# Place of the turned work and of operand sums behind the weight pieces, with one more buffer, in a two-layer fp32 decoder

## The chip, the cores and the metric

The kernel runs on one core of one Trainium2 chip. Five engines work side by side: TensorE (PE in the profile, with PEld for its weight loads), VectorE (DVE), ScalarE (ACT), GpSimd (POOL) and SyncE (SP). Each takes its own instructions strictly in order. The metric is the device time of one execution, in microseconds (us), median over runs.

## The reference

A decoder of two layers on 256 tokens of width 2048, all in float32. Layer one mixes tokens by gated linear attention (GLA, 4 heads), layer two by causal softmax attention (16 heads); each is followed by a gated feed-forward block with a causal convolution of width 3. Cut to what the change touches:

```python
def gla_mixer(x, ...):
    q, k, v, g = split(rms_norm(x) @ w_in)
    ...                                  # decays, masked scores, values
    o = rms_norm(o, o_norm_w) * silu(g)
    return o @ w_out

def conv_ffn(x, norm_w, w_up, conv_w, conv_b, w_down):
    h = rms_norm(x, norm_w) @ w_up       # 2048 -> 2 * 5632
    acc = conv_b + sum(conv_w[j] * h shifted by 2 - j tokens for j in 0..2)
    a, u = split(acc)
    return (silu(a) * u) @ w_down        # 5632 -> 2048
```

## The kernel before

Nearly all time is matrix products of 256 tokens with weights that come from HBM once, 1 MB at a time (SP issues them, L95, into three buffers `wraw`). Each megabyte holds two **pieces** of 128x1024. A piece is split into two parts of reduced precision: ACT casts it to `whi` (L132), DVE subtracts to get `wlo` (L133), and PE multiplies whi with both parts of the activations and wlo with one. One plain piece is one **step** of 12 matmuls of 512 columns (L281 and L284). `prefetch` traces the casts two pieces ahead of the step, in the down projections three to five.

The down projections (`w_go` after GLA, `w_dn` after each feed-forward block, `w_mo` after attention; matmuls at L692) save products: a megabyte marked `+` in `ORDERS` is multiplied in seven products where others take eight. It needs sums of weight blocks (`t13`, `t24`, made by DVE in `_sums`, L105 to L107, and cast and subtracted as further pieces) and sums of activation blocks (`comb`, made by `combine`, L568 to L571, and split at L294 and L295). For the feed-forward blocks the combs of `EARLY` are made as the activations come out; the others in `combine_parts` (L578 first), at places 2, 4, 6, ... of the down projection's list.

Products come out with tokens on partitions; what follows needs features there. So each result of a step group is scaled to `tok` (ACT; L600 for the gates, L623 for the up projection), transposed in blocks by DVE into `z` (L372, L624), stored to DRAM and loaded back **turned** by POOL's DMA queue (L375 and L381, L628 and L634). Then a job works on the turned tile: `keys`, `queries`, `gated` (ACT L589 into `g`, then split into `go`) and `convolve` (ACT L642, DVE L644 to L649, split into `hid`). `after(n, job)` traces a job n steps later; jobs on turned tiles have n = 6 and more. In GLA `gla_scores` (matmuls `sT`, L526) and `gla_values` (`o`, L543) come 8 and 10 steps behind the queries, the second head of a pair two steps later.

A scheduler then orders the traced instructions on each engine by its own estimate of when operands are there. So the order on an engine may differ from the order of the code, within the dependencies and within the edges that `issue_after` adds: it holds what is traced inside it behind a given instruction on that instruction's engine.

Tiles `slot` are 4 KB per partition from a pool `big` of 34.

## Time and profile before

| what | us |
|---|---|
| median of 3 runs (2234.88 to 2238.73) | 2235.11 |
| the profiled execution | 2234.8 |
| its span, first to last instruction | 2233.0 |
| TensorE busy | 2192.9 |
| VectorE busy | 1585.1 |
| ScalarE busy | 1270.8 |
| mean granted TensorE clock | 0.992 |

The profiled execution lies 0.3 us under the median and has 1.8 us outside its span. The page of the profile lists busy time, the chain of work that ended last and the costliest groups; the trace behind it tells for each instruction how long its engine sat idle ahead of it and what ended that, in square brackets. Such an idle time ahead of a matmul is time of the whole kernel, since PE is the engine that is nearly always busy. PE has few of them, 36 us in all; they stand in the GLA block and at the start of each down projection.

### The profile page before, as it was taken

Reading aid. Unit: us, or ns where it says so; the run is one execution under the profiler, and the core shown is the slowest. Engines: PE = TensorE matmul, PEld = TensorE weight load, DVE = VectorE, ACT = ScalarE, POOL = GpSimd, SP = SyncE. Lnnn points to the kernel's source line nnn. Section 1 sums busy time; section 2 is a strip of 40 time slices with the busy share of each in tenths; the row PEclk is TensorE's granted clock in tenths of the full one; section 3 lists DMA queues with packets and bytes.
Section 4 is the critical chain, followed back from the end, with each engine's and each line's share of the span. In section 5 each row is a group of like instructions: output and inputs, shape, how many; then the busy total and the mean of one; then the engine's idle time right before and its main releaser. Section 6 shows DMA issues by size and latency. Waiting matters only on the chain.

```text
span 2233.0 us, 26994 instructions
## 1 busy us (share of the span) xinstructions
PE 2192.9 (98%) x9805; PEld 1810.5 (81%) x9805; DVE 1585.1 (71%) x2162; ACT 1270.8 (57%) x1812; POOL 263.0 (12%) x368
## 2 busy tenths in 40 slices
PE   9999979999999999999999999999999999999999
PEld 7887857888888888788878888888888888887887
DVE  6655568577767767978856666776676767779886
ACT  6555545565655656555556666555565565655453
POOL 1011111111111111000021000011111111110000
PEclk9999999999999999999999999999999999999999
DMA  8576657777777787566685444486777777774655
GB/s 315 172 224 188 205 173 247 214 242 240 244 243 242 234 249 235 192 220 215 225 284 207 172 169 170 171 253 209 250 238 238 245 242 244 235 241 186 219 215 169
DMA packets 87238, 495.40 MB, mean 222 GB/s; under 512 B 12433, under 2 KB 12961, under 8 KB 37058
## 3 DMA queue, kind: packets, MB, share of 16 engines
q1 hardware_dynamic: 60578, 417.53, 53.9%
q0 software_dynamic: 25952, 75.59, 13.3%
q8 instruction: 76, 1.25, 0.2%
q10 hardware_dynamic: 576, 0.58, 0.1%
q14 instruction: 56, 0.46, 0.1%
HBM read 455.88 MB, written 37.77 MB: 221 GB/s over the span
## 4 chain that ended last, share of the span: by engine, by line
PE 82%; issue 12%; DMA 4%; DVE 1%; POOL 1%; ACT 0%; SPq 0%; DVEq 0%; POOLq 0%; ACTq 0%
PE acc L281 41%; PE acc L284 21%; PE acc L692 11%; PE p L692 7%; DMA c<-rows 1%; DMA wraw<-w_go 1%; DMA turned<-z 1%; DVE wlo L133 1%; POOL upT L634 0%; DMA turned<-queries 0%; PE sT L526 0%; PE o L543 0%; DMA wraw<-w_v 0%; DMA turned<-gates 0%; PE tr L849 0%
## 5 line engine op out<-in xcount | busy, mean ns | idle before, releaser
L133 DVE TENSOR_TENSOR wlo<-wraw,whi 128x1024 fp32r<-128x1024 f32 (+1 forms) x786 | 929.0, 1191 | 458.9 <-ACT whi L132 440.2
L132 ACT CAST whi<-wraw 128x1024 fp32r<-128x1024 f32 (+1 forms) x786 | 799.6, 1027 | 688.5 <-PE acc L281 435.3
L281 PE MATMUL acc<-whi,xw 128*128 128x512 f32 x3840 | 953.7, 390 | 3.6 <-ACT xw L244 1.9
L281 PEld LDWEIGHTS acc<-whi,xw 128*128 128x128 f32 x3840 | 720.8, 188 | 154.7 <-ACT xw L244 3.0
L284 PE MATMUL acc<-wlo,xw 128*128 128x512 f32 x1920 | 514.9, 389 | 0.0
L284 PEld LDWEIGHTS acc<-wlo,xw 128*128 128x128 f32 x1920 | 360.2, 188 | 74.7
L692 PE MATMUL acc<-whi,hid 128*128 128x512 f32 x572 | 185.2, 393 | 2.5 <-DVE c L733 2.5
L692 PE MATMUL p<-whi,hid 128*128 128x512 f32 x506 | 167.5, 393 | 0.0
L281 PE MATMUL acc<-whi,xkv 128*128 128x512 f32 x512 | 133.9, 394 | 0.0
L634 POOL DMA_DIRECT2D upT<-turned x176 | 114.0, 654 | 147.1 <-DMA turned<-z 64.5
L692 PE MATMUL acc<-whi,comb 128*128 128x512 f32 x328 | 109.2, 397 | 20.8 <-ACT whi L132 16.6
L692 PEld LDWEIGHTS acc<-whi,hid 128*128 128x128 f32 x572 | 108.2, 190 | 26.0 <-DVE c L733 3.4
L132 ACT CAST whi<-t 128x1024 fp32r<-128x1024 f32 x82 | 85.3, 1051 | 76.6 <-PE p L692 41.5
L628 POOL DMA_DIRECT2D turned<-z x44 | 34.1, 774 | 679.1 <-DVE z L624 633.0
L133 DVE TENSOR_TENSOR wlo<-t,whi 128x1024 fp32r<-128x1024 f32 x82 | 99.4, 1219 | 19.8 <-PE p L692 9.9
L692 PEld LDWEIGHTS p<-whi,hid 128*128 128x128 f32 x506 | 96.2, 190 | 20.3
L281 PEld LDWEIGHTS acc<-whi,xkv 128*128 128x128 f32 x512 | 94.1, 188 | 18.3
L642 ACT ACTIVATE au<-upT,cs 128x256 f32<-128x256 f32 x176 | 96.0, 595 | 15.8 <-DMA upT<-turned 15.7
L692 PE MATMUL acc<-wlo,hid 128*128 128x512 f32 x286 | 94.8, 390 | 0.0
L692 PEld LDWEIGHTS acc<-whi,comb 128*128 128x128 f32 x328 | 62.5, 191 | 35.9 <-ACT whi L132 18.4
L692 PE MATMUL p<-wlo,hid 128*128 128x512 f32 x253 | 83.8, 390 | 0.0
L724 POOL DMA_DIRECT2D c<-rows x24 | 21.3, 1100 | 520.1 <-DVE c L719 508.2
(241 smaller groups left out, 1931.2 us busy)
## 6 DMA issues: line engine op xcount, KB each, us to landing
wraw<-w_up SPq DMA_DIRECT2D x176, 1024.0 KB, 5.3
wraw<-w_dn SPq DMA_DIRECT2D x88, 1024.0 KB, 5.2
turned<-z POOLq DMA_DIRECT2D x44, 512.0 KB, 3.5
upT<-turned POOLq DMA_DIRECT2D x176, 128.0 KB, 4.9
wraw<-w_g SPq DMA_DIRECT2D x16, 1024.0 KB, 5.1
wraw<-w_go SPq DMA_DIRECT2D x16, 1024.0 KB, 6.1
wraw<-w_mq SPq DMA_DIRECT2D x16, 1024.0 KB, 6.1
wraw<-w_kk SPq DMA_DIRECT2D x16, 1024.0 KB, 4.9
```

The costliest lines, as they stand in the source:

```text
L132: nc.scalar.copy(hi[:, a:b], src[:, a:b])
L133: nc.vector.tensor_sub(lo[:, a:b], src[:, a:b], hi[:, a:b].bitcast(F32))
L281: T.matmul(ps[:, t, :], xs(kt)[:, x0 + 128 * t:x0 + 128 * t + 128], hi[:, c:c + 512], start=kt == 0 and x0 == 0, stop=False)
L284: T.matmul(ps[:, t, :], xs(kt)[:, 128 * t:128 * t + 128], lo[:, c:c + 512], start=False, stop=kt == KT - 1)
L628: nc.gpsimd.dma_start(turned[J].rearrange("(a i) r q c -> (i r) a (q c)", a=4), z.rearrange("p (a q) t c -> p a (q t c)", a=4))
L634: nc.gpsimd.dma_start(f[32 * q:32 * q + 32].rearrange("p a (i c) -> p (a i) c", i=4), turned[J][:, :, q, :].rearrange("a r c -> r a c"))
L642: A.activation(au[:, i, :], t[:, i, :], AF.Identity, bias=col(cb + n), scale=col(cw + 2 * 2 * FT + n))
L692: T.matmul(p[n], x[xi], w[wi][:, 512 * f:512 * f + 512], start=n not in begun, stop=left[n] == 0)
L724: nc.gpsimd.dma_start(r[n], res(n // 2, 2 * b + n % 2), accum_op=OP.add)
```

## The change

Four edits. `behind` puts jobs on turned tiles under edges to the latest traced cast (ACT) and subtraction (DVE), and those jobs are traced one step later (7 for 6). GLA's scores and values come off that list and are placed by themselves: 11 and 14 steps behind the queries for the first head, 13 and 16 for the second (8, 10, 10 and 12 before). The combs of the down projections are traced two places ahead of the megabyte that uses them, instead of at places 2, 4, 6, ...; number 7 joins `EARLY`. `big` has 35 slots.

```diff
-EARLY = (1, 3, 5)
+EARLY = (1, 3, 5, 7)
...
+        self.latest = []
...
+    def behind(self):
+
+        stack = ExitStack()
+        for ins in self.latest:
+            stack.enter_context(self.tc.issue_after(ins))
+        return stack
...
                 with self.tc.issue_after(self.first) if n + a else nullcontext():
-                    nc.scalar.copy(hi[:, a:b], src[:, a:b])
-                nc.vector.tensor_sub(lo[:, a:b], src[:, a:b], hi[:, a:b].bitcast(F32))
+                    one = nc.scalar.copy(hi[:, a:b], src[:, a:b])
+                two = nc.vector.tensor_sub(lo[:, a:b], src[:, a:b], hi[:, a:b].bitcast(F32))
+            self.latest = [one.ins, two.ins]
...
-    big = ctx.enter_context(tc.tile_pool(name="big", bufs=34))
+    big = ctx.enter_context(tc.tile_pool(name="big", bufs=35))
...
+            def run(job):
+                with ws.behind():
+                    job(got["f"])
+
             for lag, job in jobs:
-                after(lag, lambda job=job: job(got["f"]))
+                after(lag, lambda job=job: run(job))
...
-        through(g, z, [(6 + i, lambda f, hd=2 * g + i, i=i: keys(hd, f[:, 2 * i:2 * i + 2])) for i in range(2)])
+        through(g, z, [(7 + i, lambda f, hd=2 * g + i, i=i: keys(hd, f[:, 2 * i:2 * i + 2])) for i in range(2)])
...
-            jobs += [(6 + i, lambda f, hd=hd, i=i: queries(hd, f[:, 2 * i:2 * i + 2])),
-                     (8 + 2 * i, lambda f, hd=hd: gla_scores(hd)),
-                     (10 + 2 * i, lambda f, hd=hd: gla_values(hd))]
+            jobs += [(7 + i, lambda f, hd=hd, i=i: queries(hd, f[:, 2 * i:2 * i + 2]))]
+            after(11 + 2 * i, lambda hd=hd: gla_scores(hd))
+            after(14 + 2 * i, lambda hd=hd: gla_values(hd))
...
-        through(hd, z, [(6 + i, lambda f, c=2 * hd + i: gated(c, f)) for i in range(2)])
+        through(hd, z, [(7 + i, lambda f, c=2 * hd + i: gated(c, f)) for i in range(2)])
...
             au = temp("au")
+            with ws.behind():
+                for i in range(2):
+                    n = i * FT + j
+                    A.activation(au[:, i, :], t[:, i, :], AF.Identity, bias=col(cb + n),
+                                 scale=col(cw + 2 * 2 * FT + n))
             for i in range(2):
                 n = i * FT + j
-                A.activation(au[:, i, :], t[:, i, :], AF.Identity, bias=col(cb + n),
-                             scale=col(cw + 2 * 2 * FT + n))
...
-                after(6 + 2 * i, lambda J=J, i=i: convolve(2 * J + i, f[J][:, 2 * i:2 * i + 2, :]))
+                after(7 + 2 * i, lambda J=J, i=i: convolve(2 * J + i, f[J][:, 2 * i:2 * i + 2, :]))
...
-            for i, k in enumerate(new):
-                todo.setdefault(i if name == "mo" else 2 + 2 * i, []).append(
-                    lambda k=k: combine_parts(k, xs, combos))
+            for k in new:
+                at = next(i for i, (k_, _) in enumerate(order) if k_ == k)
+                todo.setdefault(max(at - 2, 0), []).append(lambda k=k: combine_parts(k, xs, combos))
```

The line numbers move down by 8 at L132, by 9 at L294, by 13 at L589 and L600, by 14 at L642 and by 16 at L718.

**The end of GLA on ACT.** This is ACT's queue where the last gate group ends and the output projection `w_go` begins. `g` is turned work (megabytes 4 and 5 of the gated result), `tok` empties the last gate group out of PSUM, `wraw_2271` is the second megabyte of w_go, `wraw_2305` the third, `t13_2307` and `t24_2308` sums of the second (in the rows of the change too). Before:

```order
L132 CAST whi_2373<-t13_2307 128x1024
L132 CAST whi_2423<-wraw_2305 128x1024
L589 ACTIVATE g_2338<-turned_2246,cs_85 128x256 x2
L589 ACTIVATE g_2362<-turned_2246,cs_85 128x256 x2
L600 ACTIVATE tok_2390<-acc_2214,col_n_524 128x512
L600 ACTIVATE tok_2394<-acc_2214,col_n_524 128x512
L294 CAST go_2341<-g_2338 128x2x256
L132 CAST whi_2344<-wraw_2271 128x1024
```

After, the same place:

```order
L140 CAST whi_2338<-wraw_2271 128x1024
L602 ACTIVATE g_2356<-turned_2246,cs_85 128x256 x2
L140 CAST whi_2322<-wraw_2271 128x512
L303 CAST go_2359<-g_2356 128x2x256
L140 CAST whi_2367<-t13_2307 128x1024
L613 ACTIVATE tok_2384<-acc_2200,col_n_524 128x512
L613 ACTIVATE tok_2388<-acc_2200,col_n_524 128x512
L140 CAST whi_2423<-wraw_2305 128x1024
```

Two of the four `g` moved from ahead of tok to behind it; the two that stay ahead stand two weight pieces earlier than before, behind the wide piece of the second megabyte.

**The first half of w_go on ACT, some ten pieces on.** `t24_2369` (before) and `t24_2363` (after) are the same sums, of the fourth megabyte; `wraw_2348` and `wraw_2342` the fifth megabyte, `wraw_2448` the sixth, `wraw_2468` the seventh. Before:

```order
L132 CAST whi_2464<-wraw_2320 128x1024
L132 CAST whi_2540<-wraw_2448 128x1024
L132 CAST whi_2562<-wraw_2468 128x1024
L589 ACTIVATE g_2487<-turned_2439,cs_85 128x256 x2
L589 ACTIVATE g_2509<-turned_2439,cs_85 128x256 x2
L294 CAST go_2490<-g_2487 128x2x256
L132 CAST whi_2493<-t24_2369 128x1024
L294 CAST go_2512<-g_2509 128x2x256
L132 CAST whi_2531<-wraw_2348 128x1024
```

After:

```order
L140 CAST whi_2464<-wraw_2320 128x1024
L140 CAST whi_2487<-t24_2363 128x1024
L140 CAST whi_2540<-wraw_2448 128x1024
L140 CAST whi_2562<-wraw_2468 128x1024
L602 ACTIVATE g_2503<-turned_2439,cs_85 128x256 x2
L602 ACTIVATE g_2525<-turned_2439,cs_85 128x256 x2
L734 COPY c0_2572<-acc_2450 128x512
L303 CAST go_2506<-g_2503 128x2x256
L303 CAST go_2528<-g_2525 128x2x256
L140 CAST whi_2531<-wraw_2342 128x1024
```

The cast of t24 moved ahead of the casts of the sixth and seventh megabyte; the second piece of the fifth megabyte (`whi_2531`) still stands behind them and behind the turned work.

**The start of a feed-forward down projection on DVE.** These rows end with the second sum of `t24` of the second `+` megabyte (number 3). `whole` and `comb` are the combs of activations, `au` and `hid` the last convolutions. Before:

```order
L568 TENSOR_TENSOR comb_7310<-whole_7308 128x128
L570 TENSOR_TENSOR comb_7310<-whole_7308 128x128
L578 TENSOR_TENSOR whole_7396<-hid_6023 128x512
L106 TENSOR_TENSOR t24_7149<-t13_7148,wraw_7043 128x512
L133 TENSOR_TENSOR wlo_7205<-t13_7148,whi_7204 128x1024
L569 TENSOR_TENSOR comb_7310<-comb_7310,whole_7308 128x128
L133 TENSOR_TENSOR wlo_7187<-wraw_7043,whi_7186 128x1024
L105 TENSOR_TENSOR t13_7237<-wraw_7167 128x1024
L568 TENSOR_TENSOR comb_7398<-whole_7396 128x128
L570 TENSOR_TENSOR comb_7398<-whole_7396 128x128
L295 TENSOR_TENSOR hid_7082<-au_7129,hid_7082 128x256
L107 TENSOR_TENSOR t24_7149<-wraw_7043,t24_7149 128x512
```

After:

```order
L107 TENSOR_TENSOR t24_7137<-t13_7136,wraw_7041 128x512
L584 TENSOR_TENSOR comb_7366<-whole_7364,comb_7366 128x128
L141 TENSOR_TENSOR wlo_7165<-wraw_7041,whi_7164 128x512
L662 SCALAR_TENSOR_TENSOR au_7125<-upT_6993,cs_85,au_7125 128x254
L582 TENSOR_TENSOR comb_7454<-comb_7454,whole_7452 128x128
L141 TENSOR_TENSOR wlo_7175<-wraw_7041,whi_7174 128x1024
L662 SCALAR_TENSOR_TENSOR au_7125<-upT_6993,cs_85,au_7125 128x254
L141 TENSOR_TENSOR wlo_7193<-t13_7136,whi_7192 128x1024
L108 TENSOR_TENSOR t24_7137<-wraw_7041,t24_7137 128x512
```

The third megabyte's first sum (`t13_7237`, 128x1024) moved behind this place, and so did part of the combs. Counted from the subtraction of the half piece of the first `+` megabyte to the row that ends each piece, the new order has 4 `whole` down to 3, 13 additions of 128x128 down to 7, one split of a comb down to none, two sums of 128x1024 down to one, two more small steps of the convolution down to one each, and seven subtractions of a full piece in both. In the up projections the place of each instruction against the weight pieces is the same as before, but for the comb of number 7.

## The prediction

> **What bounds the kernel now.** I read the engines' busy time first, then whom PE waits for, then the five stretches in which its waits lie.
>
> ```profile
> PE 2192.9 (98%) x9805; PEld 1810.5 (81%) x9805; DVE 1585.1 (71%) x2162; ACT 1270.8 (57%) x1812; POOL 263.0 (12%) x368
> PE acc L692 <- ACT whi L132: 16.6, 3, 10.9
> PE acc L692 <- ACT tok L600: 4.1, 1, 4.1
> PE acc L692 <- DVE wlo L133: 3.9, 8, 1.0
> PE sT L526 <- DVE qq L496: 1.9, 1, 1.9
> PE sT L526 <- DVE qq L498: 0.8, 1, 0.8
> ```
>
> PE is the bound, and 27.3 us of its waits stand in these five rows (total, times, longest). The change adds and removes no matmul, so all it can win is waits and what hangs on them. The next view has, for a stretch, the busy time and count of each engine, the granted clock, the DMA share and GB/s: first a quiet stretch of an up projection, then the scores of GLA, the end of GLA with the start of w_go, and the starts of the two feed-forward down projections.
>
> ```profile
> 420.00:520.00 100.00, 100.00 (x443) 82.81 (x442) 69.26 (x98) 56.77 (x79) 14.26 (x21) 1.00 0.74 235
> 184.40:205.50 21.10, 18.36 (x78) 15.25 (x77) 9.88 (x15) 9.28 (x17) 1.05 (x2) 0.84 0.57 176
> 275.60:341.00 65.40, 49.22 (x200) 39.21 (x199) 40.71 (x48) 33.32 (x48) 8.04 (x10) 0.90 0.54 162
> 915.00:935.00 20.00, 15.70 (x55) 11.66 (x55) 19.06 (x31) 10.91 (x13) 0.00 (x0) 0.83 0.45 166
> 2022.00:2042.00 20.00, 15.96 (x57) 12.04 (x58) 19.79 (x32) 10.91 (x13) 0.00 (x0) 0.83 0.45 172
> ```
>
> In quiet 100 us hold 443 matmuls, 0.226 us each, at clock 1.00: nothing to win there. At that pitch the third stretch would need 200 x 0.226 = 45.2 us and takes 65.4: 20.2 us are lost. The fourth loses 20.0 - 55 x 0.226 = 7.6, the fifth 7.1. The clock in them is 0.84 to 0.90: after a wait PE runs at half clock for a while, so a wait costs more than itself. That is the pot of the change, some 40 us.
>
> **Part 1, scores later.** Here and below a row of the timeline has start, duration, instruction and count, and in brackets the idle time ahead.
>
> ```profile
> 189.15 1.09 PE L526 MATMUL sT<-qq,kie 128*128 128x64 f32 x8 [1.89 <-DVE qq L496]
> 193.63 3.60 PE L281 MATMUL acc<-whi,xw 128*128 128x512 f32 x8
> 198.00 2.00 PE L281 MATMUL acc<-whi,xw 128*128 128x512 f32 x8
> ```
>
> The first head's scores wait 1.89 and 0.8 us for the queries; then eight matmuls take 3.60 us where the next eight take 2.00. Together 1.89 + 0.8 + 1.6 = 4.3 us. The queries come one step later (12 x 0.226 = 2.7 us), the scores three (8.1 us): 5.4 us more room than now, against waits of 2.7. All of it should go, **4.3 us**. The values come at step 14 where the first gate group ends at 16, so they still are ahead of its tok.
>
> The new ACT order mixes Silu and Exp and has two more table loads, which lie beside matmuls.
>
> ```profile
> 222.76 1.05 ACT L132 CAST whi<-wraw 128x1024 fp32r<-128x1024 f32 x1 [0.80 <-ACT qq L497]
> 223.83 1.28 ACT L600 ACT_TABLE_LOAD   x1
> 225.13 1.26 ACT L600 ACTIVATE tok<-acc,col_n 128x512 f32<-128x512 f32 x2
> ```
>
> A load costs 1.30 us (223.83 to 225.13). Behind the cast of 222.76 ACT now does a copy, two loads, tok, four steps of the values (2.2 us by the same steps at their old place) and an exponential, 6.8 us; the next cast ends near 231.6, and PE wants it near 233.7. So I take nothing for the loads, and 1 us if that room is wrong. The Trainium skill, page "ScalarE: Activation LUTs", section "What ACT_TABLE_LOAD costs", puts a switch at 2.66 us with a drain of 1.38; by it the two would take 2.7 us more, an estimate, and PE would wait 0.6 us. The row shows no drain behind the load, and I go by the row.
>
> **Part 2, the end of GLA and w_go.** How it goes now:
>
> ```profile
> 278.62 1.71 ACT L589 ACTIVATE g<-turned,cs 128x256 f32<-128x256 f32 x4 [2.69 <-DMA turned<-gates]
> 282.21 1.25 ACT L600 ACTIVATE tok<-acc,col_n 128x512 f32<-128x512 f32 x2
> 288.30 0.90 POOL L375 DMA_DIRECT2D gates<-z  x1 [16.66 <-DVE z L372]
> 305.55 1.70 ACT L589 ACTIVATE g<-turned,cs 128x256 f32<-128x256 f32 x4 [5.09 <-DMA turned<-gates]
> 307.16 1.24 ACT L600 ACTIVATE tok<-acc,col_n 128x512 f32<-128x512 f32 x2
> 308.45 1.20 PE L692 MATMUL acc<-whi,comb 128*128 128x512 f32 x4 [4.14 <-ACT tok L600]
> 315.56 0.89 POOL L375 DMA_DIRECT2D gates<-z  x1 [16.35 <-DVE z L372]
> 327.37 1.04 ACT L132 CAST whi<-wraw 128x1024 fp32r<-128x1024 f32 x1 [7.97 <-DMA wraw<-w_go]
> 333.09 1.04 ACT L132 CAST whi<-wraw 128x1024 fp32r<-128x1024 f32 x1 [4.67 <-DMA wraw<-w_go]
> 334.04 1.70 ACT L589 ACTIVATE g<-turned,cs 128x256 f32<-128x256 f32 x4
> 336.15 1.04 ACT L132 CAST whi<-t 128x1024 fp32r<-128x1024 f32 x1
> 337.25 0.80 PE L692 MATMUL acc<-whi,comb 128*128 128x512 f32 x1 [10.86 <-ACT whi L132]
> wraw<-w_go SPq DMA_DIRECT2D x16, 1024.0 KB, 6.1
> ```
>
> Turned work that waits for its DMA holds up the tok behind it, twice: the second time PE stands 4.14 us for a PSUM buffer. Then ACT waits for two megabytes that PE doesn't need yet, and the cast of t24, which it needs, stands behind them: 10.86 us.
>
> Now the new order, on the old clock. The store of gate group 2 comes earlier: its tok stands ahead of two of the four g and of two go casts, and DVE transposes right behind it. A head's values now fall between the two gate groups, so against PE the load that ended ACT's 2.69 us is in some 4 us earlier, near 274.5; two g, a go and two casts (1.05 each) later tok runs from 277.9 to 279.1, and DVE needs 2.5 us behind it. That gives a store near 281.6 instead of 288.30. From that store to the end of the wait for the loads it was 305.5 - 288.3 = 17.2 us, so the load is in near 298.8. ACT waits for it behind a piece that is cast by 296.3, so some 2.5 us, then does two g (0.8), a half piece, go, t13 and tok: done near 302.7. PE wants that buffer at 308.45 - 4.14 = 304.3 or later. The 4.14 go. DVE is then full (sums, tok, transposes), and the subtraction of the second megabyte's t24 comes about 1.3 us after PE wants it; PE had 1.2 us of such waits there before, so this is even.
>
> The t24 of the fourth megabyte is now cast ahead of the DMA waits, so the 10.86 us in that form go too. **But what is late next** is the second piece of the fifth megabyte. It stands on ACT behind the seventh megabyte, four g that need the last gates' load, one copy and two go. The last z is stored at 309.4 instead of 315.56, by the same chain, and with 17.3 us from store to load its tile is in at 326.7. The seventh megabyte is asked for when DVE lets go of its buffer, near 316.6. It landed just ahead of 333.09, slowly, with the turned loads beside it; the last row gives 6.1 us as the median of such a DMA. Some 5 us earlier than before it lands at 328, and the cast that PE needs ends at 328 + 1.0 + 1.7 + 0.5 + 1.1 + 1.0 = 333.4. With the median it lands at 322.7, the turned tile decides, and the cast ends at 331.0. PE comes there near 322 and waits 9 to 11 us. In the trace that piece's first matmul is at 340.8. It starts 7.4 to 9.8 us earlier then, and some 2 us of half clock now fall behind this point instead of ahead of it: **6.5 us** won. Bounds: 2 if the landing is later by as much as ACT waited for it before (4.67), 15 if tile and megabyte are in before PE comes and only the casts are left to wait for.
>
> **Part 3, combs later, number 7 early.** The start of `w_dn`, in both layers alike:
>
> ```profile
> 902.11 1.22 DVE L133 TENSOR_TENSOR wlo<-wraw,whi 128x1024 fp32r<-128x1024 f32 x1
> 903.25 0.68 DVE L578 TENSOR_TENSOR whole<-hid 128x512 f32<-128x512 f32 x1
> 903.85 0.87 DVE L644 SCALAR_TENSOR_TENSOR au<-upT,cs,au 128x255 f32<-128x255 f32 x2
> 904.64 0.28 DVE L568 TENSOR_TENSOR comb<-whole 128x128 f32<-128x128 f32 x1
> 904.84 0.28 DVE L570 TENSOR_TENSOR comb<-whole 128x128 f32<-128x128 f32 x1
> 923.68 0.68 DVE L107 TENSOR_TENSOR t<-wraw,t 128x512 f32<-128x512 f32 x1
> 925.54 0.79 PE L692 MATMUL acc<-whi,comb 128*128 128x512 f32 x1 [2.87 <-ACT whi L132]
> 930.81 0.63 PE L692 MATMUL p<-whi,hid 128*128 128x512 f32 x2
> ```
>
> DVE works without a break from 902.11 until t24's second sum ends at 924.36; ACT casts it, and PE has stood 2.87 us. Start to start, a full subtraction takes 1.14 us, a `whole` 0.60, an addition 0.20, a step of the convolution 0.40. The rows of the order give in the same stretch one whole less (0.60), six additions (1.2), one split (0.60), one sum of 128x1024 (1.14) and two small steps (0.68): 4.2 us less. t24 is then ready at 920.2 and cast near 921.2. PE, without its shorter waits ahead (1.4 us of the wlo row in this stretch), comes at 922.67 - 1.42 = 921.25. So the wait ends about when PE comes. Won are 2.87 + 1.42 of waits and the half clock: 12 matmuls from 925.54 to 930.81 take 5.27 us instead of 2.71. That is 6.85 us a layer, 13.7 for both; for a rest of small waits I take **13**. The combs' remaining work (split, last additions) stands later now, where a pair of megabytes takes PE 45 x 0.226 = 10.2 us and DVE, by the same durations, 8.6 plus 0.6 to 1.8: it keeps up, barely. If it doesn't, each pair gives back its excess. Bounds 3 and 14.
>
> On the clock: the Trainium skill, page "TensorE: Matmul & The Clock Gate", section "HAM oscillation — how this bites in real kernels", asks for idle gaps above about 3.4 us before the clock drops. Here a wait of 2.87 with shorter ones ahead was enough. By the page, remaining waits below 3.4 us in part 3 would cost no half clock; by the row they may.
>
> **The rest.** In the up projections each instruction keeps its place against the weight pieces, so the edges and the later step cost nothing (behind each au stand the next casts, made two steps ahead of PE); comb 7 falls where DVE is 69% busy. The 35th slot frees no wait that the PE rows name: nothing, at most 1 us either way.
>
> **Sum.** 2234.8 - 4.3 - 6.5 - 13 = 2211.0 us for the profiled execution, whose own time is 0.3 under the median.
>
> **Rivals.**
> *Only GLA heals.* The combs' additions are still hoisted to the first `+` megabytes by the scheduler, so DVE stays full and the starts of w_dn win nothing: 2234.8 - 10.8 = 2224. For it: three wholes still stand there. Against: the count of 4.2 us.
> *The wait in w_go does not come back.* If the seventh megabyte and the turned load land early, part 2 wins 15: 2202. Against it: the same loads collided before.
> *w_go gives back all.* New ACT waits for turned loads (g two pieces earlier) and table loads eat part 2: 2234.8 - 17.3 = 2217.5. The wait moves from one piece to another, as 9 to 11 us for 10.86 already suggest.
> *Change without effect, 2235.* The scheduler had set the order of its own accord, and by other waits PE loses the same.
> *Slower, 2241.* DVE falls behind in the later pairs of w_dn, where the combs' splits now stand: four pairs in two layers. If each makes PE wait 1.2 us and run half clock as now (2.5 us), 8 x 3.7 = 30 us are lost against 24 won. It decides from 11.4 us of DVE work a pair; I count at most 10.4.
>
> **How the numbers follow.** Forecast 2211, within 2206 to 2216: 0.50. Only GLA heals: 0.14. No wait in w_go: 0.12. w_go gives back: 0.14. No effect: 0.05. Slower: 0.05. The range reaches from the second rival to just past the first and leaves out no effect and slower, 0.10, and what strays beyond: **2201 to 2225**. About 0.2% (4.5 us) is what a measurement of this kernel can tell from no change. Faster 0.90, same 0.05, slower 0.05.
>
> **What would show it.** Right: no wait of sT for qq; no wait of acc for tok; in w_go one wait of 9 to 11 us for whi, whose cast is a w_go piece behind four g; in 915:935 a clock of 1.00 and DVE less than 19 us busy, in both layers. Wrong: a wait for wlo or comb in the later pairs of w_dn; a wait in the gate groups behind a table load; waits in the up projections, where I expect none.

## The result and the profile after

| kernel | median, us | runs | lowest to highest |
|---|---|---|---|
| before | 2234.99 | 4 | 2229.63 to 2238.73 |
| changed | 2217.22 | 4 | 2213.76 to 2218.84 |

The changed kernel takes 0.992 of the time before, 95% interval 0.9896 to 0.9944: 17.8 us less, somewhere from 12.5 to 23.2. Its profiled execution took 2215.93 us, with a span of 2214.1 and a mean clock of 0.998; against the profiled execution of before that is 18.9 us less, where the forecast said 23.8.

The page's busy times of the changed kernel, then whom PE waits for (total, times, longest):

```profile
PE 2184.8 (99%) x9805; PEld 1804.1 (81%) x9805; DVE 1582.3 (71%) x2160; ACT 1272.4 (57%) x1814; POOL 263.5 (12%) x368
```
```profile
PE acc L708 <- ACT whi L140: 12.0, 4, 10.2
PE acc L708 <- DVE wlo L141: 3.9, 7, 1.0
PE acc L290 <- ACT whi L140: 3.0, 1, 3.0
```

The three rows for qq and tok are gone. One long wait of 10.2 us is left. The third row of waits is the start of the kernel, where the second megabyte landed 1.2 us later than in the profile of before; the instructions up to there are the same.

The same four windows in the changed kernel (start and end, length, busy time and count of PE, PEld, DVE, ACT and POOL, then the granted clock, the DMA share and GB/s):

```profile
184.40:205.50 21.10, 21.10 (x110) 18.02 (x110) 12.21 (x17) 10.41 (x14) 4.02 (x5) 1.00 0.79 238
275.60:341.00 65.40, 53.56 (x221) 42.66 (x220) 42.36 (x49) 30.57 (x40) 11.58 (x14) 0.92 0.66 197
915.00:935.00 20.00, 19.75 (x87) 16.00 (x86) 18.75 (x26) 12.04 (x15) 0.00 (x0) 1.00 0.59 220
2022.00:2042.00 20.00, 20.00 (x90) 16.55 (x89) 19.34 (x25) 12.32 (x14) 0.00 (x0) 1.00 0.60 218
```

Three of the four are now as quiet as an up projection, at clock 1.00; the second still loses time and clock. But the program has moved under the windows, by up to 19 us at the last one. A fairer measure: both kernels run the same 9805 matmuls, so I counted them in order of their starts and took the time from one count to the next. Counts 100 to 900 hold the scores, 1100 to 1500 the end of GLA and the first columns of w_go, 1500 to 1700 its second columns; 3800 to 4000 is the start of the first layer's w_dn, 8800 to 9000 that of the second. Stretches that are the same in all kernels (900 to 1100: 40.7 to 40.9 us; 1700 to 3800: 474.6 or 474.7) are left out. All runs of the experiments stand here too. A row is the one profiled execution of its kernel, and that isn't always near the median of its runs: those of e1, e2 and e3 are the second fastest of theirs, that of e12 is the fastest, that of e10 the slowest.

```
us between the starts of the matmuls with these numbers (0: the start of the span)
              0-100  100-900  1100-1500  1500-1700  3800-4000  4000-4900  4900-8800  8800-9000  9000-9804
before         28.9    181.8      110.9       43.7       53.3      203.4      854.2       52.8      184.3
changed        30.1    176.0      105.8       43.7       49.1      203.1      854.2       47.7      184.8
e1             30.9    176.0      109.3       43.7       47.3      204.0      854.2       47.8      185.2
e2             28.9    176.0      103.9       43.7       50.4      203.0      854.1       51.5      187.0
e3             29.3    176.0      107.4       46.3       53.2      204.6      854.1       51.9      187.3
e4             32.0    176.0       94.4       48.1       50.2      203.9      854.1       49.1      185.8
e5 (before)    30.6    176.0      109.4       43.7       52.9      203.5      854.1       52.6      185.0
e6             31.4    176.0      103.0       43.7       45.4      208.3      857.9       45.5      194.2
e7             29.2    176.0      107.2       43.7       47.3      205.3      854.0       47.7      186.7
e8             29.0    176.0       94.9       48.1       46.5      206.9      857.7       46.8      191.7
e9             31.1    176.0       92.3       46.2       48.9      204.5      854.2       48.1      185.5
e10            30.1    176.0       94.5       45.3       49.7      204.8      854.2       48.5      186.9
e11            28.8    176.0      102.5       43.7       48.8      208.0      854.1       49.7      188.0
e12            29.2    176.0      102.0       43.7       48.4      206.1      854.0       49.6      184.8
```

So the 18.9 us are: scores 5.8, w_go 5.1, the two starts of w_dn 4.2 and 5.1 (the rest within 0.5), less 1.2 at the start of the kernel. The forecast had 4.3, 6.5 and twice 6.5.

### The profile page after: what moved, and what is told of

Read it like the earlier page. It is cut to its first block, busy times and chain, and to the rows that moved or that the text cites. A ratio compares the mean times of both kernels' runs of the same rounds, so it can differ in the third digit from the quotient of the medians.

```text
span 2214.1 us, 26964 instructions
## 1 busy us (share of the span) xinstructions
PE 2184.8 (99%) x9805; PEld 1804.1 (81%) x9805; DVE 1582.3 (71%) x2160; ACT 1272.4 (57%) x1814; POOL 263.5 (12%) x368
## 4 chain that ended last, share of the span: by engine, by line
PE 85%; issue 9%; DMA 3%; DVE 1%; ACT 1%; POOL 0%; SPq 0%; ACTq 0%; DVEq 0%; POOLq 0%
PE acc L290 44%; PE acc L293 22%; PE acc L708 10%; PE p L708 6%; DMA c<-rows 1%; DVE wlo L141 1%; DMA wraw<-w_go 0%; DMA wraw<-w_dn 0%; DMA turned<-gates 0%; PE sT L539 0%; DMA wraw<-w_v 0%; PE o L556 0%; PE tr L865 0%; PE acc L773 0%; DMA gates<-z 0%
## 5 line engine op out<-in xcount | busy, mean ns | idle before, releaser
L290 PEld LDWEIGHTS acc<-whi,xkv 128*128 128x128 f32 x512 | 94.1, 188 | 18.3
L708 PE MATMUL acc<-wlo,hid 128*128 128x512 f32 x286 | 94.9, 391 | 1.6 <-DVE wlo L141 1.5
L662 DVE SCALAR_TENSOR_TENSOR au<-upT,cs,au 128x254 f32<-128x254 f32 x176 | 80.0, 476 | 0.0
```

Of the source, the lines that this page charges most:

```text
L290: T.matmul(ps[:, t, :], xs(kt)[:, x0 + 128 * t:x0 + 128 * t + 128], hi[:, c:c + 512], start=kt == 0 and x0 == 0, stop=False)
L662: V.scalar_tensor_tensor(au[:, i, 2:], t[:, i, :S - 2], col(cw + n), au[:, i, 2:], op0=OP.mult, op1=OP.add)
L708: T.matmul(p[n], x[xi], w[wi][:, 512 * f:512 * f + 512], start=n not in begun, stop=left[n] == 0)
```

## The experiments

In the expectations below, A and B are the theories between which a run was to decide; a letter behind a result says which of them it bears out. Times of all runs; each ratio is against the kernel before on the same chip (medians 2233.3 us in 28 runs for e1 to e4, 2232.2 in 17 for e5 to e8, 2233.58 in 11 for e9 to e12).

| run | what it is | median, us (runs) | ratio, 95% interval |
|---|---|---|---|
| e1 | before + part 3 | 2225.56 (11) | 0.9972, 0.9957 to 0.9987 |
| e2 | changed without part 3 | 2221.36 (10) | 0.9947, 0.9931 to 0.9963 |
| e3 | before + scores and values later | 2235.86 (12) | 1.002, 1.0001 to 1.004 |
| e4 | changed, last gates' turned work 4 steps later | 2214.68 (4) | 0.9921, 0.9898 to 0.9944 |
| e5 | before, again | 2229.63 (1) | |
| e6 | changed, combs held in place | 2227.31 (12) | 0.9975, 0.9963 to 0.9987 |
| e7 | changed without edges | 2218.46 (6) | 0.9944, 0.9929 to 0.9958 |
| e8 | e4 and e6 together | 2220.82 (5) | 0.9955, 0.9941 to 0.9969 |
| e9 | e4, casts of w_go in order | 2209.39 (4) | 0.9899, 0.9883 to 0.9914 |
| e10 | e9, number 9 early | 2209.39 (4) | 0.99, 0.9883 to 0.9916 |
| e11 | changed, number 7 not early | 2221.13 (5) | 0.9955, 0.994 to 0.9971 |
| e12 | changed, old comb places | 2220.54 (6) | 0.9949, 0.9932 to 0.9967 |

**e1, part 3 alone**, on the kernel before:

```diff
-EARLY = (1, 3, 5)
+EARLY = (1, 3, 5, 7)
-    big = ctx.enter_context(tc.tile_pool(name="big", bufs=34))
+    big = ctx.enter_context(tc.tile_pool(name="big", bufs=35))
...
-            for i, k in enumerate(new):
...
+                todo.setdefault(max(at - 2, 0), []).append(lambda k=k: combine_parts(k, xs, combos))
```

> The kernel before with the third part alone (combs two places ahead of use, number 7 early, 35 slots). Theory A, the parts are separate: the two starts of w_dn win what they won in the changed kernel, 4 to 6 us each, so 2224 to 2227 us against 2235 before; GLA and w_go keep their waits of 1.9, 4.1 and 10.9 us. Rival B, the later step of the turned work is needed for it, because it moves the convolutions of the last megabytes away from the first sums: under 4 us in all, 2231 or more, and PE still waits over 1.5 us for a cast near the second + megabyte of w_dn.

Measured: 2225.56, and the two starts won 6.0 and 5.0 us in the trace: A. By the interval part 3 alone is worth 2.9 to 9.6 us; the trace, of a fast execution (2220.01), has more. One thing neither theory had: in this trace no matmul of the scores waits for the queries, though GLA's instructions are those of before. And w_go's waits are 1.9 us for tok and 9.4 for the cast, where A had 4.1 and 10.9, with the same instructions too.

**e2, the rest of the change alone**: the changed kernel with the two edits of e1's first and last lines undone.

> The changed kernel with the combs of the down projections as before (old places, number 7 not early): the turned work alone. Theory A: scores win 5 to 6 us, w_go 4 to 6, the starts of w_dn nothing, so 2223 to 2226 us; the wait of 2.87 us for the cast of t24 stands in both layers. Rival B: the later convolutions crowd the start of w_dn, that wait grows past 4 us, and the time is 2229 or more.

Measured: 2221.36, a little better than A said, and A's reason is not right in all: the wait of 2.87 us is gone here too (the longest for a subtraction is 1.8), and the starts won 2.9 and 1.3 us. So the turned work's new place unloads the start of w_dn as well, and part 3 and the rest overlap there: 11.0 us of the starts alone (e1), 4.2 alone (e2), 9.3 together.

**e3, scores and values later, alone**, on the kernel before with 35 slots:

```diff
-                     (8 + 2 * i, lambda f, hd=hd: gla_scores(hd)),
-                     (10 + 2 * i, lambda f, hd=hd: gla_values(hd))]
+                     ]
+            after(11 + 2 * i, lambda hd=hd: gla_scores(hd))
+            after(14 + 2 * i, lambda hd=hd: gla_values(hd))
```

> The kernel before with GLA's scores and values 11 and 14 (13 and 16) steps behind, and 35 slots; no edges, the queries and all other turned work a step later as in the kernel before (6). Theory A: the two waits of sT for qq (1.9 and 0.8 us) and the half clock behind them go, 4 to 6 us, and nothing else changes: 2229 to 2231 us with waits of 4.1 and 10.9 us still in w_go. Rival B: the move of the values between the gate groups is what makes the tok wait go too, so that this edit alone wins 8 or more: 2227 or less.

Measured: 2235.86, no faster than before, if anything slower by up to 0.4%. Both theories fall. Its trace has no wait for the queries, but neither has that of e1, where GLA is untouched: 176.0 us for counts 100 to 900 in both. The long wait of w_go, 10.7 us, stands. The trace also has a new wait of 1.89 us for a cast in w_go's second columns, which take 46.3 us for 43.7, so what the edit may win on average in the scores could be hidden by what it loses there.

**e5, the kernel before a second time**, unchanged, because of e1 and e3:

> The kernel before, unchanged, profiled a second time. The third part alone showed no wait of sT for qq although it leaves GLA's instructions as they were. Theory A, that wait hangs on when the turned load lands in one execution, not on the kernel: here too it is under 0.5 us, or the second head has it instead of the first, and PE reaches its 1000th matmul 3 to 6 us earlier than in the first profile, with the start of the kernel taken out. Rival B, it is the kernel's and the third part changed something ahead of it: 1.5 to 2.5 us as in the first profile.

A, clearly. The row of PE at the first head's scores in this second profile, and DVE's row for the queries:

```profile
187.02 1.29 DVE L496 TENSOR_TENSOR qq<-turned,eb 128x512 f32<-128x512 f32 x2 [4.80 <-DMA turned<-queries]
188.78 1.00 PE L526 MATMUL sT<-qq,kie 128*128 128x64 f32 x8
191.13 2.10 PE L281 MATMUL acc<-whi,xw 128*128 128x512 f32 x8
```

The queries' step on DVE starts at 187.02 instead of 188.31, since the turned tile landed 1.3 us earlier, and PE comes 1.5 us later, since the kernel's start was slower. No wait, no half clock (the eight matmuls at 191.13 take 2.10 us where the first profile has 3.60), and 176.0 us where the first profile has 181.8. PE and the load arrive within 2 us of each other there, and which one is first differs from execution to execution.

**e7, no edges:** `behind` taken out of both places, all step numbers kept.

> The changed kernel without the edges (no behind), with all steps (7, 11, 14) and comb places kept. Theory A, the step numbers do the work and the edges only pin what comes out so anyway: 2215 to 2219 us, no wait of acc for tok over 1 us. Rival B, without edges the g go ahead of weight casts on ACT and wait there for their loads: the tok wait of 2 to 4 us returns at the end of GLA, and the time is 2220 or more.

Measured 2218.46, and no wait of acc for tok: A. The step numbers carry the gain; what the edges add is not more than the intervals can hide.

**e4, the last gate group's turned work later**, on the changed kernel:

```diff
-        through(hd, z, [(7 + i, lambda f, c=2 * hd + i: gated(c, f)) for i in range(2)])
+        through(hd, z, [((11 if hd == 3 else 7) + i, lambda f, c=2 * hd + i: gated(c, f)) for i in range(2)])
```

It tests what the remaining 10.2 us are. In the changed kernel's timeline (start, duration, engine, instruction, idle time ahead; SPq is an issue of the weight loads):

```profile
313.01 0.33 SPq L96 DMA_DIRECT2D wraw<-w_go  x1
323.56 1.04 ACT L140 CAST whi<-wraw 128x1024 fp32r<-128x1024 f32 x1 [6.01 <-DMA wraw<-w_go]
324.51 1.70 ACT L602 ACTIVATE g<-turned,cs 128x256 f32<-128x256 f32 x4
326.11 0.56 ACT L734 COPY c<-acc 128x512 f32<-128x512 f32 x1
326.58 1.14 ACT L303 CAST go<-g 128x512 fp32r<-128x512 f32 x2
327.62 2.94 ACT L140 CAST whi<-wraw 128x1024 fp32r<-128x1024 f32 x3
328.71 1.22 PE L708 MATMUL acc<-whi,go 128*128 128x512 f32 x2 [10.16 <-ACT whi L140]
333.98 0.39 PE L708 MATMUL acc<-whi,go 128*128 128x512 f32 x1
```

The first of the three casts at 327.62 is the one PE waits for. Its megabyte had been in for long: its other piece had been cast ahead of 316. It stands behind the seventh megabyte, which took 10.4 us from its issue.

> The changed kernel with the last gate group's turned work four steps later (11 for 7), so that both pieces of the fifth and of the sixth megabyte of w_go are cast ahead of it. Theory A, the 10.2 us wait comes from the place of one cast behind the seventh megabyte, four g, a copy and two go on ACT: it goes, with its half clock, and what is late next is the first piece of the seventh megabyte with its go, under 1.5 us: 9 to 12 us won, 2204 to 2208 us. Rival B, the loads are the limit: the eighth megabyte is now asked for beside the seventh and the turned tiles, the seventh lands 4 us later or more than at 323.5, and PE waits there instead: under 6 us won.

Measured in the trace: counts 1100 to 1500 take 94.4 us instead of 105.8, 11.4 won, as A said. The next wait is one for go, 2.02 us, a little over A's bound. But the whole gain in the median is 2.5 us, inside the intervals and under the 6 that B allowed: 4.4 us came back in w_go's second columns 1.1 and 1.4 at the starts of w_dn, 0.8 and 1.0 behind them, and this execution began 1.9 us later. B's reason isn't borne out either: the seventh megabyte landed at 322.44, a little earlier than the 323.46 before the edit. ACT and PE in the second columns:

```profile
351.35 0.62 ACT L140 CAST whi<-wraw 128x512 fp32r<-128x512 f32 x1 [2.10 <-DMA wraw<-w_go]
353.94 1.04 ACT L140 CAST whi<-t 128x1024 fp32r<-128x1024 f32 x1 [1.22 <-PE acc L708]
354.89 1.04 ACT L140 CAST whi<-wraw 128x1024 fp32r<-128x1024 f32 x1
355.98 0.53 PE L708 MATMUL acc<-whi,comb 128*128 128x512 f32 x1 [2.15 <-ACT whi L140]
```

A t13 cast waits 1.22 us for a buffer that PE has to free, and the cast that PE needs stands behind it.

**e9, casts in order:** e4 with an edge from each cast of w_go to the cast of the piece before it.

```diff
-                with self.tc.issue_after(self.first) if n + a else nullcontext():
+                with self.tc.issue_after(self.latest[0] if 96 < n < 136 else self.first) if n + a else nullcontext():
```

> e4 (last gate group's turned work four steps later) with w_go's casts held in the order of its pieces by edges on ACT. In e4, PE waits 2.15 us in the second columns for a plain cast that stands behind a t13 cast which itself waits for a buffer, and 4.4 us are lost there with the clock. Theory A, it is that order: the wait falls under 0.7 us, 3 to 4.5 us won against e4's 2214.7, 2210 to 2212 us. Rival B, the megabyte comes too late whatever the order (it landed 4.7 us ahead of the wait): the wait stays over 1.5 us and the time at 2213 or more.

Measured 2209.39, in all four runs between 2208.23 and 2209.83: A, a little better; the longest wait for a cast is 0.7 us. Counts 1100 to 1700 take 138.5 us here, 142.5 in e4, 149.5 in the changed kernel. The window that held the long wait, and the rows of waits for casts and go:

```profile
275.60:341.00 65.40, 63.93 (x283) 52.27 (x282) 48.10 (x57) 37.52 (x52) 13.32 (x17) 1.00 0.77 248
```
```profile
PE acc L708 <- ACT whi L140: 1.8, 3, 0.7
PE acc L708 <- ACT go L303: 0.5, 1, 0.5
```

283 matmuls stand where the changed kernel has 221. This kernel and e10, which has the same median, are the fastest of the study, 0.9899 of before. The edges were tried on top of e4 only, so what they do without its later place isn't known.

**e6, combs held in place**, on the changed kernel. It asks why the starts of w_dn gave 9.3 us and not 13.

```diff
-                todo.setdefault(max(at - 2, 0), []).append(lambda k=k: combine_parts(k, xs, combos))
+                def held(k=k):
+                    with ws.behind():
+                        combine_parts(k, xs, combos)
+                todo.setdefault(max(at - 2, 0), []).append(held)
```

DVE and PE at the start of w_dn in the changed kernel, first layer:

```profile
898.37 0.68 DVE L591 TENSOR_TENSOR whole<-hid 128x512 f32<-128x512 f32 x1
899.71 0.68 DVE L591 TENSOR_TENSOR whole<-hid 128x512 f32<-128x512 f32 x1
900.31 1.21 DVE L141 TENSOR_TENSOR wlo<-t,whi 128x1024 fp32r<-128x1024 f32 x1
903.58 0.68 DVE L591 TENSOR_TENSOR whole<-hid 128x512 f32<-128x512 f32 x1
904.58 2.35 DVE L141 TENSOR_TENSOR wlo<-wraw,whi 128x1024 fp32r<-128x1024 f32 x2
...
901.82 0.73 PE L708 MATMUL acc<-whi,hid 128*128 128x512 f32 x2 [0.54 <-ACT whi L140]
905.85 0.74 PE L708 MATMUL acc<-wlo,hid 128*128 128x512 f32 x2 [1.01 <-DVE wlo L141]
913.41 0.50 PE L708 MATMUL acc<-whi,comb 128*128 128x512 f32 x1 [0.65 <-ACT whi L140]
916.27 0.51 PE L708 MATMUL acc<-wlo,comb 128*128 128x512 f32 x1 [0.25 <-DVE wlo L141]
```

Three wholes stand ahead of a subtraction that PE waits 1.01 us for; the first of their combs is split for its use by ACT only at 926.67.

> The changed kernel with the whole combine_parts (whole, four additions, split) behind edges to the latest weight piece, so that nothing of it is hoisted ahead of its place. Theory A, what w_dn still loses are the wholes and additions that the scheduler puts ahead of subtractions in the first pairs: PE's waits of 0.5, 1.0, 0.7 and 0.3 us in the first layer and 0.5, 0.7, 0.3 in the second go, 3 to 4 us won, 2212 to 2214 us. Rival B, the pairs behind become full: DVE has 8.6 + 0.6 + 0.8 + 0.6 = 10.6 us of work where PE needs 10.2, so that each of eight pairs in the two layers loses 0.4 us and in part its clock: new waits for wlo or comb from the third pair on, and 2217 to 2225 us.

Both are right, each at its place. The starts win 3.7 and 2.2 us more than in the changed kernel (45.4 and 45.5), as A said: 15.2 us against the kernel before, more than the 13 of the forecast. And B decides the time: 5.2 us are lost in the rest of the first w_dn, 3.7 between the blocks (all of it at the start of attention's output projection, which makes its combs in the same function) and 9.4 in the rest of the second: 2227.31, more than the 2217 to 2225 that B had. One of these losses, on DVE, ACT and PE:

```profile
954.78 0.29 DVE L584 TENSOR_TENSOR comb<-whole,comb 128x128 f32<-128x128 f32 x1
954.99 1.23 DVE L106 TENSOR_TENSOR t<-wraw 128x1024 f32<-128x1024 f32 x1
956.32 1.04 ACT L140 CAST whi<-t 128x1024 fp32r<-128x1024 f32 x1 [0.59 <-DVE t L106]
957.42 0.97 PE L711 MATMUL acc<-whi,comb 128*128 128x512 f32 x3 [2.03 <-ACT whi L140]
```

The comb's additions push back a weight sum, its cast comes late, and PE stands 2.03 us.

**e8, e4 and e6 together:**

> e6 and e4 together: held combs and the last gate group's turned work four steps later. Theory A, the sets of waits are separate, so both gains add: e4 won 11 us in the first columns of w_go against the changed kernel and gave 4 back in the second columns, whose megabytes then come too late; with 3 to 4 us from w_dn the time is 2209 to 2212 us. Rival B, what is won upstream is lost downstream to loads and DVE: 2214 or more.

Measured 2220.82: B. w_go keeps its gain (94.9) and the starts theirs (46.5, 46.8), the losses behind them stay (206.9, 857.7, 191.7).

**e10, number 9 early as well**, on e9: `EARLY = (1, 3, 5, 7, 9)`.

> e9 with number 9 early too (five combs made in the up projections). Theory A, what the starts of w_dn still lose is DVE work that can be done in the up projections, where DVE is 71% busy: one comb less there is 0.6 + 0.8 us less at the start and 0.6 less in a later pair, PE's waits before its 4000th and its 9000th matmul fall by 1 to 2 us in each layer, 2 to 4 us in all against e9. Rival B, the scheduler fills the room with the next comb (as it does now), so that the waits only change their place: within 1.5 us of e9.

Measured 2209.39, as e9: B. The starts take 49.7 and 48.5 us where e9 has 48.9 and 48.1; the three wholes ahead of the subtractions are still there, of the next three combs, and PE still waits 0.73 and 1.00 us there. But these two traces differ in one landing besides: the ACT step of the last convolution, which waits for its turned tile, starts 24.8 and 19.5 us behind the matmuls 3800 and 8800 in e10, 23.4 and 18.6 in e9. In e4 it starts as late as in e10, and against e4 (50.2 and 49.1) the comb made early has won 0.5 and 0.6 us, less than A's 1 to 2.

**e11 and e12, the halves of part 3:** e11 is the changed kernel with `EARLY = (1, 3, 5)`, e12 with the combs at places 2, 4, 6, 8.

> The changed kernel with EARLY (1, 3, 5) as before: of the third part only the later places. Theory A, the places bring the gain: between the 1600th and the 4000th matmul and between the 4900th and the 9000th the trace gains 3 to 5 us each on the kernel before, as the changed kernel does (4.2 and 5.1); 2216 to 2219 us. Rival B, the comb made early brings it: here under 2.5 us each, as with the turned work alone (2.9 and 1.4), and 2220 to 2222 us.

> The changed kernel with the combs at the old places 2, 4, 6, 8 and number 7 early: of the third part only that comb. Theory A, the places bring the gain: under 2.5 us in each of the two stretches named for the run before, 2220 to 2222 us. Rival B, the comb made early brings it: 3 to 5 us each, 2216 to 2219 us.

The expectations pull apart here. By the trace each half alone wins 3 to 5 us at each start (e11: 4.5 and 3.1; e12: 4.9 and 3.2), which both theories had only for one of them. By the medians, 2221.13 and 2220.54, neither does better than e2, which has no part of it (2221.36), and both together do: 2217.22. e11 gives the gain back behind the starts, 4.6 and 3.7 us, with a new wait of 1.45 us for a cast at 931.29; a comb more has to be finished there, which by e6 would explain it. e12 gives back 2.7 in the first layer; its trace is of its lowest run (2215.25) and says less about its median, so what e12 lacks stays open. At the starts, too, part of the differences is that one landing. In the second layer ACT's step starts 17.9 to 18.1 us behind matmul 8800 in e2, e12 and the changed kernel, and counts 8800 to 9000 take 51.5, 49.6 and 47.7 us: at a like landing the early comb alone brings half of what part 3 has over e2. e11 has the step at 20.1 us and takes 49.7; what the places alone would give at 18 no run shows.

The 35th slot was not tried by itself.

## Why the prediction was right, and by how much its terms were off

The time lies in the range and the sign is right. The forecast of 2211.0 was too low by 4.9 us against the profiled execution and by 6.2 against the median, and its terms were off in both directions. That it came so near is luck in part: against e5, the second profile of the kernel before (2229.63), the same execution of the changed kernel is only 13.7 us faster, not 18.9.

**What bounds the kernel.** Right: PE has 9805 matmuls before and after, and all that was won is waits and clock.

**Part 1, "all of it should go, 4.3 us".** In the profile it went, and was 5.8. But the wait doesn't belong to every execution of the kernel before. Thirteen later profiles, two of them with GLA's code of before (e1, e5), have 176.0 us there, and the first profile alone has 181.8. The step that failed is the first: to take 1.89 and 0.8 us of waits from one execution for what each has. e3 made the edit alone and won nothing, with a loss in w_go that may hide a part. How often the wait falls due in the kernel before, two profiles can't say. The two more table loads cost PE nothing, as forecast: loads stand at 217.22, 221.93 and 247.43, the ACTIVATE behind the first starts 1.30 us later and that behind the second 1.29, counts 900 to 1100 with the first two take 40.7 us against 40.9, and no matmul waits near the third.

**Part 2, 6.5 us.** The mechanism came as written: no wait for tok, none for t24, and one wait of 9 to 11 us (10.16) for the second piece of the fifth megabyte, behind the seventh, four g, a copy and two go. Its size was 5.1. That piece's first matmul starts at 328.71 instead of 340.8, 12.1 us earlier, of which 4.7 had been won ahead of it by count 1100: 7.4, the lower end of the 7.4 to 9.8. The seventh megabyte took 10.4 us where the forecast weighed 6.1 against a late landing. And the 12 matmuls from 328.71 to 333.98 take 5.27 us instead of 2.71, so 2.6 us of half clock and not 2. Against e5 the same term is only 3.6, and in e2, e6, e11 and e12, whose ACT and DVE instructions stand in the changed kernel's order here, the stretch takes 102.0 to 103.9 us for 105.8: the size of this term differs by some 4 us between executions. Its parts on the side of before differ as well: the wait for tok, 4.14 us in the first profile, is 2.4 in e5 and 1.9 in e1. The rival in which this wait doesn't come back was priced at 15 over before; e4 and e9, which take it away by the later place of the turned work, e9 with the casts in order besides, have 16.5 and 18.6 over before in counts 1100 to 1500, 12.1 and 16.1 with the second columns.

**Part 3, 13 us.** Right in kind: no wait of 2.87, clock 1.00 in both windows (and, since the program has moved, in counts 3800 to 4000 and 8800 to 9000, where before has 0.94), DVE 18.75 us busy in the first, less than 19. In the second it is 19.34, not less. Mis-sized: 4.2 and 5.1, 9.3 together. The step that failed is the one from "4.2 us less" of DVE work to a t24 that is ready 4.2 us earlier, with the short waits gone. The work did fall: in the stretch of which the order was counted DVE was busy 22.85 us without a break (901.51 to 924.36), and is now busy 18.89. But the stretch now takes 22.03 us in the first layer (890.17 to 912.20), since DVE stands idle in it, and 20.46 in the second. The idle times of the first layer, and ACT's step between them:

```profile
891.81 1.22 DVE L141 TENSOR_TENSOR wlo<-wraw,whi 128x1024 fp32r<-128x1024 f32 x1 [0.95 <-ACT whi L140]
894.58 1.09 ACT L656 ACTIVATE au<-upT,cs 128x256 f32<-128x256 f32 x2 [2.80 <-DMA upT<-turned]
895.21 0.98 DVE L660 SCALAR_TENSOR_TENSOR au<-upT,cs,au 128x255 f32<-128x255 f32 x2 [2.18 <-ACT au L656]
```

DVE waits for a late convolution, and that for its turned tile. Behind it the scheduler has put wholes of later combs ahead of the subtractions, and PE now waits 0.54 and 1.01 us there where before it didn't, and 0.65 and 0.25 further on. The short waits of before were these, in the first layer:

```profile
915.58 0.50 PE L692 MATMUL acc<-wlo,comb 128*128 128x512 f32 x1 [0.42 <-DVE wlo L133]
920.60 0.73 PE L692 MATMUL acc<-wlo,comb 128*128 128x512 f32 x2 [0.40 <-DVE wlo L133]
921.93 0.50 PE L692 MATMUL acc<-wlo,comb 128*128 128x512 f32 x1 [0.60 <-DVE wlo L133]
```

The changed kernel has these in the second:

```profile
2006.75 0.73 PE L708 MATMUL acc<-wlo,hid 128*128 128x512 f32 x2 [0.47 <-DVE wlo L141]
2014.31 0.50 PE L708 MATMUL acc<-whi,comb 128*128 128x512 f32 x1 [0.68 <-ACT whi L140]
2017.17 0.50 PE L708 MATMUL acc<-wlo,comb 128*128 128x512 f32 x1 [0.25 <-DVE wlo L141]
```

The new waits add up to 2.45 us in the first layer and 1.40 in the second. Taken from the 6.85 us a layer of the forecast they leave 4.4 and 5.45, close to the 4.2 and 5.1 measured. How late that tile lands differs between the runs. In e7, where ACT's step starts 20.9 us behind matmul 3800 and not 23.6 as here, counts 3800 to 4000 take 47.3 us instead of 49.1; in e4, with 24.8, they take 50.2. In the five profiles without the edges of `behind` the step comes at 20.9 to 21.9, in the nine with them at 22.5 to 24.8, so the edges seem to have a part in it; how is not shown. e6 shows the hoisted work's share: with it out of the way the starts give 15.2 us, though the step comes late there too (23.1 us).

**The rival "slower", at 0.05.** It did not come true in the changed kernel, whose later pairs lose nothing. But its mechanism is real, and the price of 30 us was the right order: in e6 DVE does fall behind: 14.6 us are lost behind the two starts of w_dn and 3.7 in attention's output projection, 18.3 in all. The forecast counted 8.6 plus 0.6 to 1.8 us of DVE work in a pair and said it keeps up, barely. It keeps up because the scheduler does a part of it early, the same part that costs the starts 5.9 us. "Only GLA heals" was near to this, but the starts win in spite of the hoisted work.

**"w_go gives back all", 2217.5.** The time is as if it had come true, the trace says it didn't: w_go won 5.1.

**The clock.** The waits that are left in part 3, up to 1.01 us, cost no half clock. The forecast had left that open.

**The rest.** Counts 1700 to 3800, nearly all of the first up projection, take 474.6 us before and after: nothing, as forecast. The 1.2 us at the start of the kernel were in no term; over these fourteen profiles count 100 falls between 28.8 and 32.0 us, with the same instructions ahead of it.

## What to carry to other kernels

A wait in one profile is the property of one execution until a second profile shows it: where a load and its user arrive within a few us of each other, profile twice before pricing it, and compare two kernels at like landings. Work that is moved later frees its old place only if nothing else is hoisted into that; and where the engine is nearly full behind, hoisting is what keeps it from falling behind, so pinning the work at its place can cost more than it frees. On the engine that makes the casts, let them stand in the order in which they are needed, ahead of anything that waits for a transfer. At the one place where this was tried, after the change had only moved the wait, both steps together won 7.8 us by the medians (2217.22 to 2209.39), though the intervals of the two ratios just overlap: the later place of the turned work alone 2.5, the order of the casts on top of it 5.3.

## What the runs showed of the hardware

The clock does not follow from a wait's length alone. In e4 PE stood 2.02 us ahead of 325.44 and 2.15 ahead of 355.98; in e6 it stood 2.03 ahead of 957.42 (shown with e6). The first of the two rows of e4, then the windows behind the three waits (the granted clock is the number after the five engines):

```profile
325.44 0.69 PE L708 MATMUL acc<-whi,go 128*128 128x512 f32 x1 [2.02 <-ACT go L303]
```
```profile
325.40:336.00 10.60, 10.56 (x39) 8.58 (x40) 9.19 (x12) 5.99 (x10) 4.15 (x5) 0.84 0.82 170
355.90:368.00 12.10, 12.02 (x46) 9.74 (x47) 11.55 (x12) 9.36 (x12) 0.00 (x0) 0.86 0.73 258
```
```profile
953.00:973.00 20.00, 17.86 (x77) 13.81 (x76) 18.39 (x26) 11.47 (x13) 0.00 (x0) 1.00 0.43 161
```

By 0.226 us a matmul the first two lose 10.56 - 39 x 0.226 = 1.7 and 12.02 - 46 x 0.226 = 1.6 us while PE is busy, the third 0.5. The Trainium skill, page "TensorE: Matmul & The Clock Gate", section "HAM oscillation — how this bites in real kernels", asks for idle gaps above about 3.4 us; these runs have the drop at 2.02, and none at 2.03. What else decides it stays open.

With the same instructions the start of the kernel differs by 3.2 us between executions (count 100 at 28.8 to 32.0), and the landing of the first head's queries by 1.3 us between the two profiles of the kernel before. The kernel before ran from 2224.71 to 2242.87 us in 28 runs, the kernel of e9 in four from 2208.23 to 2209.83.
